# Input projections by seven block products in front, prompt heads in pairs on halves of the array, and gate and merge weights through ACT's queue

## The chip, the cores and the metric

The kernel runs on one core of a Trainium2 chip. Its time is the device time of one execution in microseconds (us). PE is the matrix engine (PEld its weight loads), DVE, ACT and POOL the vector, scalar and general engines; SP issues DMAs, and so can ACT.

## The reference, cut to what matters

One layer of a streaming encoder on 1024 prompt frames and 8 x 16 sample frames (1152 rows of 1024 features, nine row tiles of 128). Everything is fp32.

```
z = rmsnorm(x) @ w_in          # qa ka va | qb kb vb (512 columns each) | fl (8) | qm (512) | gates (3 x 1024)
qa, ka, qb, kb, qm = per-head rmsnorm of their columns; mk, mv = rmsnorm(mem) @ w_mkv
A: chunk-band attention with a learned bias, 8 heads x 64     B: causal attention with forget gates, 8 heads x 64
M: attention into 256 memory rows, 4 heads x 128              samples: the same three against 512 cached rows each
x = x + (sum over b of sigmoid(gate_b) * (o_b @ w_pb)) @ w_o
x = x + relu(rmsnorm(x) @ w_up)^2 @ w_down
```

## The kernel before, in words

Each fp32 product is made of fp32r products: an operand is split into a high part (a copy on ACT, `hilo` and `split`) and a low part (source minus high, on DVE or POOL), and hi.hi + hi.lo + lo.hi are summed in PSUM (`mm3`). The stages, in time:

- **Front.** Columns V_A, Q_A, the memory keys and values, K_A and V_B (with the eight forget columns), each as nine row tiles x 8 contraction blocks x 3 matmuls (`group`). V_B is 520 wide and goes as two banks of 260 columns, the others as one of 512. `head_norm` and `to_T` norm a tile (ACT square, DVE sum, POOL root in `rstd`, DVE scale, gain) and transpose it on PE.
- **Attention A, samples A, attention B, samples B, attention M, samples M** (`attend` with `prompt_ab`, `sample_ab`, `prompt_m`, `sample_m`). A planner (`Plan`) fixes the order here: it walks in planned time, keeps a clock for each engine from `COST`, for the DMAs in `load`, for PE in `pe.matmul`, and emits the first task whose inputs are ready; when none is, it emits one step of a **filler**. What it emits is kept in that order on every engine. The fillers are, one after another: `project` (Q_B, K_B and Q_M in halves of 256 columns, 1296 matmuls), `gates` (24 feature tiles x 72 matmuls of 384 columns), `merge` (24 x 36 of 384 columns).
- **Rest.** What is left of gates and merge, then W_o and the two feed-forward products, which the change leaves alone.

In `prompt_ab` a head is 64 wide. `prepare` loads its keys twice, one copy under the other, and its queries as 64 rows of high over 64 rows of low parts, so two 128-row matmuls give one piece of scores (`scores`: `qs` with `kh`, `qs` with `kl`). `soften` adds the bias and takes the row minimum on DVE, `exp_norm` does exp on ACT and the division; `transposes` turns the probabilities on PE and splits them (`turn`: ACT high, DVE low); `values` multiplies each 128-key block with `vs`, high and low values side by side, for the high and the low part (two matmuls of up to 256 columns), and `out` adds the two halves.

In `sample_ab`, fp32 matmuls are used as they are, on four column tiles of the array (`tile_position=(0, 32 * pr)`).

The weights of gates and merge are fetched by `staged`: one staging buffer for the gates, the DMA on SP's queue, then `split`. SP's queue carries the cached keys and values of the samples as well, in the order of the plan.

## Time and profile before

| | us |
|---|---|
| runs: median of 3 (lowest to highest) | 2049.38 (2044.78 to 2052.18) |
| profiled execution | 2052.52 |
| its span | 2050.7 |
| PE busy / weight loads busy | 1994.0 / 1817.3 |
| DVE / ACT / POOL busy | 1214.4 / 965.6 / 568.4 |

PE is busy for 97% of the span; a matmul's record lasts longer than its share of the pipeline, so the distance from one start to the next tells what one costs, and busy time only where PE stood still. The mean granted clock is 0.994 of 2.4 GHz. The chain that ended last is PE's for its last 17%, and shows nothing of the stages ahead of it.

### The profile page before, as it was taken

What the parts mean: (1) busy time and instruction counts of PE and PEld (TensorE: products, weight loads), DVE (VectorE), ACT (ScalarE), POOL (GpSimd) and SP (SyncE); (2) the same over time, 40 slices, a digit from 0 to 9 for tenths busy, and PEclk for the clock granted to TensorE, in tenths of its full rate; (3) what the DMA queues carried; (4) which work ended last, traced back from release to release, by engine and by line L of the source; (5) the groups of instructions that cost most, each with busy time, mean ns of one, the idle gap of its engine ahead of it and who ended that gap; (6) DMA issues with size and microseconds to landing.
All of it is one profiled execution on the core that took longest, in us unless ns stands there. A gap on an engine that the chain in (4) does not pass through costs nothing. (4 is left out here: it accounts for less than half of the span.)

```text
span 2050.7 us, 35667 instructions
## 1 busy us (share of the span) xinstructions
PE 1994.0 (97%) x12946; PEld 1817.3 (89%) x12946; DVE 1214.4 (59%) x2383; ACT 965.6 (47%) x1950; POOL 568.4 (28%) x650
## 2 busy tenths in 40 slices
PE   9999999999899998899999999989999999999999
PEld 7778999999599997698989997889999998888887
DVE  3444178886269882254254662696555655785775
ACT  6443268886357772254242122564444454453332
POOL 2435066664134551110021010235344431000000
PEclk9999999999999999999999999999999999999999
DMA  8453155554964437745375443225343449663463
GB/s 287 137 176 122 62 136 135 148 131 125 296 179 125 123 92 238 246 131 199 132 246 179 130 144 118 67 92 178 131 144 130 140 157 318 196 200 110 127 194 127
DMA packets 227374, 325.54 MB, mean 159 GB/s; under 512 B 48101, under 2 KB 120950, under 8 KB 227198
## 3 DMA queue, kind: packets, MB, share of 16 engines
q1 hardware_dynamic: 176888, 281.85, 43.9%
q10 hardware_dynamic: 50310, 41.42, 6.5%
q8 instruction: 102, 1.67, 0.4%
q14 instruction: 74, 0.61, 0.1%
HBM read 238.00 MB, written 85.18 MB: 158 GB/s over the span
## 5 line engine op out<-in xcount | busy, mean ns | idle before, releaser
L1625 PE MATMUL b<-r 128*128 128x512 f32 (+2 forms) x2200 | 457.5, 357 | 5.3 <-ACT r L199 3.0
L1625 PEld LDWEIGHTS b<-r 128*128 128x128 f32 x2200 | 379.7, 190 | 63.5 <-ACT r L199 3.9
L199 ACT ACTIVATE r<-fa 128x512 fp32r<-128x512 f32 (+4 forms) x264 | 212.1, 813 | 330.4 <-PE b L1625 281.2
L199 DVE TENSOR_TENSOR r<-fa,r 128x512 fp32r<-128x512 f32 (+4 forms) x264 | 271.5, 1039 | 138.9 <-ACT r L199 133.9
L210 PE MATMUL z<-hi,whi 128*128 128x384 f32 x960 | 300.4, 345 | 10.9 <-ACT whi L199 9.5
L1625 PE MATMUL b<-r,r 128*128 128x320 f32 (+1 forms) x1928 | 288.3, 299 | 4.8 <-DVE r L199 4.7
L1625 PEld LDWEIGHTS b<-r,r 128*128 128x128 f32 x1928 | 271.2, 190 | 6.6 <-DVE r L199 6.6
L210 PE MATMUL z<-hi,wlo 128*128 128x384 f32 x768 | 259.5, 338 | 0.5
L210 PE MATMUL z<-whi,hi 128*128 128x256 f32 (+2 forms) x792 | 255.7, 324 | 1.8 <-DVE lf L199 0.8
L210 PE MATMUL z<-wlo,hi 128*128 128x256 f32 (+2 forms) x792 | 248.6, 314 | 1.9 <-DVE wlo L199 0.9
L210 PE MATMUL z<-whi,lo 128*128 128x256 f32 (+2 forms) x792 | 247.4, 313 | 0.0
L199 POOL TENSOR_TENSOR fa<-fa 128x512 f32<-128x512 f32 x114 | 167.7, 1478 | 246.6 <-ACT fa L199 126.3
L210 PEld LDWEIGHTS z<-hi,whi 128*128 128x128 f32 x960 | 178.5, 189 | 20.7 <-ACT whi L199 12.1
L210 PE MATMUL z<-lo,whi 128*128 128x384 f32 x576 | 194.0, 337 | 0.0
L199 ACT ACTIVATE whi<-wst 128x512 fp32r<-128x512 f32 (+1 forms) x160 | 99.5, 629 | 195.3 <-DMA wst<-in_w_g 72.4
L210 PEld LDWEIGHTS z<-wlo,hi 128*128 128x128 f32 x792 | 150.2, 190 | 14.1 <-DVE wlo L199 3.2
L210 PEld LDWEIGHTS z<-whi,hi 128*128 128x128 f32 x792 | 149.8, 189 | 12.9 <-ACT whi L199 2.5
L210 PEld LDWEIGHTS z<-whi,lo 128*128 128x128 f32 x792 | 149.8, 189 | 9.4 <-DVE lo L199 0.4
L199 DVE TENSOR_TENSOR wlo<-wst,whi 128x512 fp32r<-128x512 f32 (+1 forms) x127 | 96.4, 771 | 102.8 <-ACT whi L199 102.1
L210 PEld LDWEIGHTS z<-hi,wlo 128*128 128x128 f32 x768 | 144.9, 189 | 2.6 <-DVE wlo L199 2.6
L199 ACT ACTIVATE s<-s,nm 128x256 f32<-128x256 f32 (+8 forms) x180 | 122.3, 681 | 41.3 <-DVE nm L199 38.3
L199 POOL TENSOR_SCALAR s<-s,ri 128x640 f32<-128x640 f32 (+8 forms) x100 | 78.1, 783 | 183.9 <-DVE ri L199 148.3
(190 smaller groups left out, 3401.8 us busy)
## 6 DMA issues: line engine op xcount, KB each, us to landing
td<-fa SPq DMA_DIRECT2D x112, 256.0 KB
fa<-td SPq DMA_DIRECT2D x80, 256.0 KB
fa<-in_w_down SPq DMA_DIRECT2D x76, 256.0 KB
fa<-in_w_up SPq DMA_DIRECT2D x32, 512.0 KB
tg<-tg ACTq DMA_DIRECT2D x72, 192.0 KB
th<-tg SPq DMA_DIRECT2D x72, 192.0 KB
wst<-in_w_in SPq DMA_DIRECT2D x48, 256.0 KB
wst<-in_w_g SPq DMA_DIRECT2D x48, 256.0 KB
```

Source lines behind the costliest of these rows:

```text
L199: ins = f(*a, **k)
L210: ins = nc.tensor.matmul(out, lhsT, rhs, **k)
L1625: pin(nc.tensor.matmul(ps, lh, rh, **k))
```

## The change

**Projections.** `project`, `group` and the fillers made of them go. V_A with the forget columns (520 wide) comes first as before V_B did. The other six column groups go in three pairs (Q_A, K_A), (V_B, Q_B), (K_B, Q_M). For a pair, an even and an odd row tile and the two halves of the contraction are a 2 x 2 block product, which `products` makes of seven block products (S1 to S4 are sums of blocks of x from `sums`, T the sums of weight blocks from the sources in `makers_of`); the ninth row tile is made straight. Weights stand in seven slots, each filled again by `release`; `in_order` keeps PE and DVE in the order written. `norm` runs in steps, each some row tiles behind (`in_`). Memory keys and values follow. All this stands ahead of attention A, and the fillers are gates and merge alone.

**Prompt heads in pairs.** In `prompt_ab` two heads lie in the two halves of the 128 rows. A piece of scores is three matmuls for each head (hi.hi, hi.lo, lo.hi) on 64 rows of the array, head by head in turn, into two banks. The values are one fp32 matmul for each head and key block, on 64 columns of the array. The transposed probabilities are one fp32 copy, on ACT or DVE.

**Queue.** `staged` issues its DMA on ACT's queue, which the planner counts apart (`dma2`). The planner also counts a matmul on a part of the array with that part's share.

```diff
-            plan.now += n * ((2 if "tile_position" in k else 4) if rhs.dtype == F32 else 2 if n < 256 else 1) / 2400 + 0.003
+            side = 128 * 128 // (lhsT.shape[0] * out.shape[0]) if "tile_position" in k else 1
+            plan.now += n * (4 if rhs.dtype == F32 else 2 if n < 256 else 1) / side / 2400 + 0.003
...
+    UW, NR, NW = HB + 8, 10, 7
+    RW, WA, SA = arena(prj, "rw", NR * UW), arena(prj, "wa", 2 * NW * UW, F32R), arena(prj, "sa", 4096, F32R)
...
+    def sums(t):
+
+        x = x_place(t)
+        e0, e1, o0, o1 = x[:, 0:4, 0:P], x[:, 4:8, 0:P], x[:, 0:4, P:], x[:, 4:8, P:]
+
+        def scale(kh):
+            y = x[:, 4 * kh:4 * kh + 4, :]
+            return lambda: vec.tensor_tensor(y, y, gcol[:, 0, 4 * kh:4 * kh + 4, None].to_broadcast((P, 4, 256)), ALU.mult)
+
+        def s1():
+            vec.tensor_tensor(o1, o0, o1, ALU.add)
+            hilo(o1, S1[:, t, 0], S1[:, t, 1])
+
+        def s2():
+            vec.tensor_tensor(o1, o1, e0, ALU.subtract)
+            hilo(o1, S2[:, t, 0], S2[:, t, 1])
+
+        def s3():
+            vec.tensor_tensor(o0, e0, o0, ALU.subtract)
+            into_odd(t, o0)
+
+        def s4():
...
+    def makers_of(pair, after):
...
+        def m2(k):
+            def source():
+                b, back = take()
+                vec.tensor_tensor(kept[k], b, kept[k], ALU.subtract)
+                back()
+                return take()
+            return source
+
...
+        queue.extend([x for k in ks for x in (R(k), L(4 + k))] + [R(4 + k) for k in ks] + [L(k) for k in ks]
+                     + [R(4 + k) for k in ks] + [R(k) for k in ks] + [L(4 + k) for k in ks])
+        makers.extend([m(k) for m in (m1, m2, m6, m7, m5) for k in ks] + [take] * 8 + [m4(k) for k in ks])
...
+    def run(u0, tiles, ks=range(4), free=True):
+
+        for x, (lhs, key, first, last, then) in enumerate(tiles):
+            put_lo()
+            if first:
+                zs[key] = zbank()
+            ps = zs[key]
+            for k in ks:
+                (h, l), (wh, wl) = lhs(k), (w[:, :HB] for w in wt[u0 + k])
+                pe.matmul(ps, h, wh, start=first and k == ks[0], stop=False, skip_group_check=True)
+                pe.matmul(ps, h, wl, start=False, stop=False, skip_group_check=True)
+                pe.matmul(ps, l, wh, start=False, stop=last and k == ks[-1], skip_group_check=True)
+                if free and x == len(tiles) - 1:
+                    release(u0 + k)
+            if then:
+                then(ps)
+            if len(ks) > 1:
+                flush()
+
...
+        r = tl(pj, (P, 8), tag="hr", bufs=4)
+
+        def sums():
+            q = tl(pj, (P, 8), tag="hss", bufs=4)
+            vec.tensor_reduce(q[:, :nh], v3(sq), AX.X, ALU.add)
+            rstd(q[:, :nh], r[:, :nh], dh)
+            gps.tensor_scalar(r[:, :nh], r[:, :nh], sc, 1.0, ALU.mult, ALU.mult)
+            in_(2, scale)
+
+        def scale():
+            zn = tl(pj, (P, HB), tag="zn") if fresh else z
+            vec.tensor_tensor(v3(zn), v3(z), r[:, :nh, None].to_broadcast((P, nh, dh)), ALU.mult)
+            if gain is not None:
+                vec.tensor_tensor(v3(zn), v3(zn), gain[:, None, :].to_broadcast((P, nh, dh)), ALU.mult)
...
+        run(u0, [(even(t), t, True, True, copy(u3[t])) for t in ts] + [(last, "s", True, False, None)])
+        run(u0 + 4, [(upper(last), "s", False, True, beside(left))]
+            + [(upper(even(t)), "y", True, True, m2(t)) for t in ts])
+        run(u0 + 8, [(of(S2, t), t, False, True, copy(u2[t])) for t in ts])
+        run(u0 + 12, [(odd_(t), t, False, True, copy(u3[t])) for t in ts])
+        run(u0 + 16, [(of(S1, t), "y", True, True, both(t)) for t in ts])
+        for t in ts:
+            if hook:
+                hook(t)
+            run(u0 + 20, [(of(S4, t), "y", True, True, plus(u2[t], lambda: right(2 * t, u2[t])))], free=False)
+            run(u0 + 24, [(last, "s", t == 0, False, None)], (t,))
+        run(u0 + 20, [(upper(last), "s", False, True, beside(right))])
+        if hook:
+            for t in ts:
+                hook(4 + t)
+        run(u0 + 28, [(upper(odd_(t)), t, False, True, copy(u2[t], lambda t=t: left(2 * t + 1, u2[t]))) for t in ts])
...
+    in_order.extend((pe, vec))
+    in_(8, rs_T)
+    for n, step in enumerate(sums(3)):
+        in_(n + 1, step)
+    products(8, q_out("a", 64), k_out("a"))
+    products(40, v_out(o["vb"], rs), q_out("b", 64))
+    products(72, k_out("b"), q_out("m", 128), at_last)
...
-        sp.dma_start(st, src)
-        t = plan.load(256)
+        act.dma_start(st, src)
+        t = plan.load(256, "dma2")
...
-        UK, NL, NS = (3, 1, 3) if b == "a" else (4, 2, 4)
+        UK, NS, NU, NB = (3, 6, 8, 3) if b == "a" else (4, 5, 7, 3)
...
+                    qh, ql, kh, kl = heads[p][:4]
+                    ks, qc, ps = slice(k0 * P + x, k0 * P + x + m), slice(blk * P, (blk + 1) * P), []
+                    for e in range(2):
+                        if x == 0:
+                            ss_[n, e] = tl(pool, (P, WK), tag="s", bufs=NS)
+                        ps.append((plan.take("s"), tl(psum["s"], (P, 512), tag="s")))
+                    for j, (q, k) in enumerate(((qh, kh), (qh, kl), (ql, kh))):
+                        for e in range(2):
+                            r = slice(64 * e, 64 * e + 64)
+                            pe.matmul(ps[e][1][:, :m], q[r, qc], k[r, ks], start=j == 0, stop=j == 2, tile_position=(64 * e, 0))
+                    for e in range(2):
+                        plan.spawn(soften(e, ps[e][1], ps[e][0], x, m, x + m == nkey))
...
+                k = plan.first(m * P, ("act", 0), ("vec", 0.2))
+                if k == "act":
+                    act.activation(dst, t[:, 0:m, :], AF.Copy)
+                else:
+                    vec.tensor_copy(dst, t[:, 0:m, :])
+                t_ = plan.op(k, m * P)
...
+                pv, vd = tl(psum["pv"], (P, 512), tag="pv")[:, 0:256], heads[p][4]
+                for m, (kb, a, z) in enumerate(plan_):
+                    for e in range(2):
+                        pe.matmul(pv[64 * e:64 * e + 64, a * P:z * P], vd[:, kb, 64 * e:64 * e + 64],
+                                  units[p, g][e][u][:, r, a * P:z * P], start=m == 0, stop=m == len(plan_) - 1, tile_position=(0, 64 * e))
...
-    plan.bufs = dict(z=2, tp=3, s=2, pv=1)
+    plan.bufs = dict(z=2, tp=2, s=3, pv=1)
```

On PE, in the projections. Before, among the fillers, one row tile of Q_B (`z`; `whi`, `wlo` are weight parts, `hi`, `lo` parts of x):

```order
L210 MATMUL z_2616<-wlo_1969,hi_145_213 128x256
L210 MATMUL z_2616<-whi_1968,lo_150_218 128x256
L217 MATMUL tp_2639<-ident_203,lf_210 72x128
L210 MATMUL z_2616<-whi_1968,hi_145_213 128x256
L210 MATMUL z_2616<-wlo_1969,hi_145_213 128x256
L210 MATMUL z_2616<-whi_1968,lo_151_219 128x256
```

Now, in the front, the product with S4 (in `sb`) of the first pair, the weights in `wa`; `fe` holds normed results on their way to a transposition:

```order
L215 MATMUL z_1629<-wa_256,sb_264 128x512 x12
L222 MATMUL tp_1646<-ident_203,fe_268 128x128 x4
L215 MATMUL z_1621<-wa_256,hi_163_231 128x512 x2
L215 MATMUL z_1621<-wa_256,lo_166_234 128x512
L215 MATMUL z_1669<-wa_256,sb_264 128x512 x12
```

1296 matmuls of 256 columns are gone from the fillers, and those of 512 columns in the front are 1248 where they were 744.

On PE, in attention A, a score piece of 512 columns. Before:

```order
L210 MATMUL s_3310<-kh_2928,qs_2930 128x512
L210 MATMUL s_3310<-kl_2929,qs_2930 128x512
```

Now:

```order
L215 MATMUL s_4185<-kh_3835,qh_3837 128x512
L215 MATMUL s_4187<-kh_3835,qh_3837 128x512
L215 MATMUL s_4185<-kl_3836,qh_3837 128x512
L215 MATMUL s_4187<-kl_3836,qh_3837 128x512
L215 MATMUL s_4185<-kh_3835,ql_3838 128x512
L215 MATMUL s_4187<-kh_3835,ql_3838 128x512
```

Two heads took four matmuls of a piece, and take six, in three rounds. In A and B together there are 96 such pieces of two heads, and PE passes 247 times between the whole array and a part of it.

On the queues, in samples A (`kd`, `vd`, `v` are cached keys and values, `wst` the gates' staging buffer). SP before:

```order
L199 DMA kd_7191<-in_cak 128x512 x4
L199 DMA kd_7271<-in_cak 128x512 x4
L199 DMA wst_7325<-in_w_g 128x512
L199 DMA kd_7364<-in_cak 128x512 x4
L199 DMA v_1780_7091<-out_va 16x512
L199 DMA vd_7392<-in_cav 128x512 x4
```

SP now, and behind it ACT a little later, in attention B:

```order
L203 DMA kd_6694<-in_cak 128x512 x4
L203 DMA kd_6747<-in_cak 128x512 x4
L203 DMA v_1240_6344<-out_va 16x512
L203 DMA vd_6813<-in_cav 128x512 x4
L203 DMA kd_6833<-in_cak 128x512 x4
```

```order
L203 ACTIVATE s_7512,sm_7597<-s_7512,nm_7567 128x896
L203 ACTIVATE s_7514,sm_7611<-s_7514,nm_7570 128x896
L203 DMA wst_7633<-in_w_g 128x512
L203 ACTIVATE pt_7584<-tp_7628 128x4x128
L203 ACTIVATE pt_7585<-tp_7643 128x4x128
```

The weights left SP's queue, and stand on ACT between the exp of the scores and the copies of the transposed probabilities. On PE, 210 matmuls of fillers stood between the first score of samples A and the first of attention B, and 318 do now; between samples B and attention M 255, and now 372.

## Rows read from the trace of the kernel before

**Rows 1.** Busy time by stage: front, A, samples A, B, samples B, the rest.

```profile
core 0: us, PE busy (x) PEld busy (x) DVE busy (x) ACT busy (x) POOL busy (x), PEclk, DMA share, GB/s
0.00:293.40 293.40, 288.15 (x1659) 248.93 (x1660) 114.91 (x198) 131.73 (x248) 105.44 (x125) 1.00 0.49 153
293.40:507.70 214.30, 212.79 (x1768) 210.63 (x1770) 177.56 (x549) 167.20 (x441) 129.74 (x186) 1.00 0.50 133
507.70:588.00 80.30, 69.71 (x712) 54.27 (x711) 23.82 (x77) 23.95 (x60) 9.21 (x18) 0.98 0.81 255
588.00:791.30 203.30, 203.11 (x1376) 197.86 (x1376) 165.74 (x462) 143.90 (x333) 95.85 (x132) 1.00 0.46 129
791.30:889.80 98.50, 83.15 (x752) 65.82 (x752) 26.22 (x79) 26.36 (x63) 8.42 (x22) 0.95 0.77 243
...
960.90:1213.10 252.20, 243.95 (x1517) 233.68 (x1517) 128.47 (x232) 70.39 (x138) 29.62 (x27) 0.99 0.55 175
```

**Rows 2.** Timeline of PE in the front: start us, duration us, instruction.

```profile
22.03 0.39 PE L210 MATMUL z<-wlo,hi 128*128 128x512 f32 x1
22.26 0.40 PE L210 MATMUL z<-whi,lo 128*128 128x512 f32 x1
```

**Rows 3.** Timeline of PE in attention A: values, then scores.

```profile
352.88 0.28 PE L210 MATMUL pv<-ptl,vs 128*128 128x256 f32 x1
353.00 0.22 PE L210 MATMUL pv<-pth,vs 128*128 128x128 f32 x1
353.05 0.28 PE L210 MATMUL pv<-ptl,vs 128*128 128x128 f32 x1
353.17 0.33 PE L210 MATMUL s<-kh,qs 128*128 128x256 f32 x1
```

**Rows 4.** Timeline of the weight loads (PEld) there.

```profile
353.00 0.19 PEld L210 LDWEIGHTS pv<-ptl,vs 128*128 128x128 f32 x1
353.11 0.19 PEld L210 LDWEIGHTS s<-kh,qs 128*128 128x128 f32 x1
```

**Rows 5.** Timeline of PE in samples A: scores, fillers, values, transpositions.

```profile
556.62 1.10 PE L210 MATMUL s<-kd,qb 128*32 128x264 f32 x16
557.65 0.44 PE L210 MATMUL z<-hi,whi 128*128 128x384 f32 x1
557.93 0.34 PE L210 MATMUL z<-lo,whi 128*128 128x384 f32 x1
558.10 0.34 PE L210 MATMUL z<-hi,wlo 128*128 128x384 f32 x1
...
558.62 0.34 PE L210 MATMUL z<-hi,wlo 128*128 128x384 f32 x1
558.89 1.08 PE L210 MATMUL pv<-vd,spt 128*32 128x128 f32 x32
559.79 0.40 PE L210 MATMUL pv<-v,t 128*32 128x128 f32 x8
560.12 0.77 PE L217 MATMUL tp<-ident,s 128*128 128x128 f32 x5
560.64 0.42 PE L210 MATMUL z<-hi,whi 128*128 128x384 f32 x1
```

**Rows 6.** What PE waited for: first line samples A, the others samples B.

```profile
PE s L210 <- DMA kd<-in_cak: 5.4, 6, 1.5
...
PE s L210 <- DMA kd<-in_cbk: 5.0, 6, 1.9
PE z L210 <- ACT whi L199: 4.4, 1, 4.4
```

**Rows 7.** Groups of DVE and POOL: busy us, mean ns, idle before and releaser.

```profile
L199 DVE TENSOR_TENSOR wlo<-wst,whi 128x512 fp32r<-128x512 f32 x119 | 88.1, 748 | 100.9 <-ACT whi L199 100.1 <-issue 0.2
...
L199 POOL TENSOR_TENSOR hr<-hr,mhalf 128x8 f32<-128x8 f32 x18 | 29.5, 1639 | 1.5
```

**Rows 8.** The gates' stores on ACT's queue: issue ns (min/median/max), first and last us.

```profile
L199 ACTq DMA_DIRECT2D tg<-tg x72: 320/326/1142, 514.6 to 1061.8; - x72
```

More of the change, by code (lines that the diff above doesn't have):

```diff
@@ L188, in tile_encoder @@
     plan = Plan()
+    in_order = []
     class Engine:
@@ new lines, in tile_encoder, with prepare, put_lo, produce @@
+    wt, makers = [], []
+    sources, los = [], []
+    def prepare(u):
+        if len(sources) <= u < len(makers):
+            sources.append(makers[u]())
+    def put_lo():
+        while los:
+            los.pop(0)()
+    def produce(place, lo_now=None):
+        u = len(wt)
+        prepare(u)
+        put_lo()
+        if u == len(makers):
+            return
+        src, then = sources[u]
+        h, l = (x[:, :src.shape[1]] for x in place)
+        act.activation(h, src, AF.Copy)
+        wt.append(place)
+        def lo():
+            (lo_now or vec).tensor_tensor(l, src, f32(h), ALU.subtract)
+            if then:
+                then()
+        los.append(lo)
+        if lo_now:
+            put_lo()
+        else:
+            prepare(u + 1)
@@ new lines, in release, with ask, take, back @@
+    def release(u):
+        if u != NW:
+            produce(wt[u])
+    queue, asked, taken, used = [], [0], [0], set()
+    def ask():
+        while asked[0] < len(queue) and (asked[0] < NR - 4 or asked[0] - (NR - 4) in used):
+            sp.dma_start(raw[4 + asked[0] % (NR - 4)][:, :HB], queue[asked[0]])
+            asked[0] += 1
+    def take():
+        n = taken[0]
+        taken[0] += 1
+        assert n < asked[0]
+        def back():
+            used.add(n)
+            ask()
+        return raw[4 + n % (NR - 4)][:, :HB], back
@@ new lines, in k_out, with then, v_out, handle @@
+    def k_out(b):
+        def then(t, zn):
+            sp.dma_start(o["k" + b][t * P:(t + 1) * P, :], zn)
+            in_(2, lambda: to_T(zn, kT[b], t))
+        return lambda t, z: norm(z, rs[:, t:t + 1], 64, lambda zn: then(t, zn), g_of["k" + b])
+    def v_out(dst, scale, fresh=False):
+        def handle(t, *of):
+            zn = of[0] if of[0].shape[1] == HB and not fresh else tl(pj, (P, HB), tag="zn")
+            x = 0
+            for z in of:
+                act.activation(zn[:, x:x + z.shape[1]], z, AF.Copy, scale=scale[:, t:t + 1])
+                x += z.shape[1]
+            act.dma_start(dst[t * P:(t + 1) * P, :], zn)
+        return handle
@@ new lines, in tile_encoder @@
+    sp.dma_start(bf, i["b_f"].to_broadcast((P, 8)))
+    x_load(4)
+    x_split(4)
+    x_load(1, slice(0, 4))
+    x_load(1, slice(4, 8))
+    x_rows(1)
+    x_split(1)
+    x_rows(TT - 1)
+    PAIRS = ((Q_A, K_A), (V_B, Q_B), (K_B, Q_M))
+    for n, pair in enumerate(PAIRS):
+        makers_of(pair, PAIRS[n + 1] if n < 2 else None)
+    queue.extend(i["w_mkv"][k * P:(k + 1) * P, x:x + HB] for x in (0, HB) for k in range(KD))
+    makers.extend([take] * 16)
+    for k in range(4):
+        sp.dma_start(kept[k], rows_(Q_A)(k))
@@ L438, in forget_gates @@
+    mem_products(104, mem_k)
+    fes.close()
+    sbs.close()
+    pgs = ExitStack()
+    pg = pgs.enter_context(tc.tile_pool(reuse_waits="tile", name="pg", bufs=2, side="right"))
+    rb = tl(pg, (P, NT), tag="rb", bufs=1)
+    sp.dma_start(rb, rsd.to_broadcast((P, NT)))
     def forget_gates(pool):
@@ new lines, in prompt_ab, with prepare, load @@
+        kq, vb, done, bias_at = Times(), Times(), Times(), Times()
+        turned, summed = defaultdict(int), defaultdict(dict)
+        live, softs = [0], [0]
+        pvs = set()
+        def prepare(p):
+            r = slice(p * P, (p + 1) * P)
+            def load(src):
+                w = yield from plan.ring(("ld", b), 1)
+                t = tl(pool, (P, NP), tag="ld", bufs=1)
+                sp.dma_start(t, src[r, 0:NP])
+                return t, plan.load(512), w
+            kd, t, w = yield from load(kT[b])
+            kh, kl, qh, ql = (tl(pool, (P, NP), F32R, tag=x) for x in ("kh", "kl", "qh", "ql"))
+            vd = tl(pool, (P, 8, P), tag="vd")
+            heads[p] = qh, ql, kh, kl, vd, {}
+            for part in range(2):
+                yield t
+                for x, n in halves(NP):
+                    c = slice(x, x + n)
+                    yield from plan.idle("act")
+                    yield from split(kd[:, c], (kh, qh)[part][:, c], (kl, ql)[part][:, c], n)
+                plan.give(w)
+                if part == 0:
+                    kd, t, w = yield from load(qT[b])
+            kq[p] = plan.t
+            sp.dma_start(vd, o["v" + b].rearrange("(k p) c -> p k c", p=P)[:, 0:8, r])
+            vb[p] = plan.load(512)
+            if p == 0:
+                plan.spawn(prepare(1))
@@ L1555, in tile_encoder @@
     plan.filler = next(f), f
-    with tc.tile_pool(reuse_waits="tile", name="fg", bufs=1) as pool:
-        plan.spawn(forget_gates(pool))
-        plan.run([])
     def attend(name, part):
```

696 lines of the change are left out of this document (320 added, 376 removed).

## The prediction

> **What bounds the kernel now.** I read busy time by stage first. PE is the bound in nearly every stage [rows 1]: in attention A it stands idle 214.30 - 212.79 = 1.5 us, in attention B 0.2 us, with DVE, the next, at 178 and 166 us. So what the change is worth is read from PE's work, matmul by matmul. The exceptions are the two sample stages [rows 1]: PE idles 80.30 - 69.71 = 10.6 us in samples A and 98.50 - 83.15 = 15.4 us in samples B, while the DMAs carry 255 and 243 GB/s. W_o and the feed-forward part follow from 1213.1 us on, and nothing changes there.
>
> Second, what a matmul costs: the distance of starts in the timeline. In the front a 512-column matmul takes 0.23 us [rows 2]. A 256-column one takes 0.12, a 128-column one 0.05 and then 0.12, 0.085 on average [rows 3]; 384 columns take 0.17 (557.93 to 558.10) [rows 5]. So a 512-column matmul costs 0.23 where two of 256 cost 0.24.
>
> Third, parts of the array. The samples' scores are eight fp32 matmuls, 16 records, on four column tiles of 32, and take 557.65 - 556.62 = 1.03 us; the values are 20 fp32 matmuls of 128 columns, 40 records, in 560.12 - 558.89 = 1.23 us [rows 5]. The tiles run side by side: a round of four values takes about 0.226 us if 0.1 goes to the passage. That passage shows too: the first filler behind the scores is followed after 0.28 us where its fellow takes 0.17, and the last filler ahead of the values after 0.27 [rows 5]. I take 0.1 us for each passage between the whole array and a part.
>
> **The change part by part.** The profiled execution took 2052.5 us, 3.1 above the median of the runs; the sum goes against it.
>
> *Projections.* Before: 744 matmuls of 512 columns, 432 of 260 and 1296 of 256. Now 1248 of 512 (96 of them the memory's, as before), and the same 432 of 260. That is 504 x 0.23 = 115.9 us more and 1296 x 0.12 = 155.5 us less: **-39.6 us**. Seven block products for eight are 30 us of it, whole banks for half ones the rest. The transpositions stay as many.
>
> *Scores.* Before: 80, 160, 112 and 32 matmuls of 512, 384, 256 and 128 columns: 80 x 0.23 + 160 x 0.17 + 112 x 0.12 + 32 x 0.085 = 61.7 us. Now 96 pieces in three rounds of two halves: 60, 120, 84 and 24 rounds. No row shows two row halves at work. Lower end: a round costs one matmul, 47.2 us (128 columns at 0.12). Upper end: the halves follow each other, 576 matmuls, 92.7 us. I take the lower end, since the four column tiles are the nearest rows: **-14.5 us**, with -14.5 and +31.0 kept.
>
> The rule that speaks against it: the Trainium skill (TensorE: Matmul & The Clock Gate, section LDWEIGHTS) gives a weight load a time of columns / 1.2 GHz, however few rows it has, so each half's load of 128 columns would be 107 ns; by that, if the loads follow each other, a round is at least 0.213 us and the scores come to 62.4 us, which is no gain. The trace agrees for the whole array, where such loads start 0.11 us apart [rows 4]; no run here shows two loads to different rows.
>
> *Values.* Before 448 matmuls of 256 columns at 0.12 and 160 of 128 at 0.085: 67.4 us [rows 3]. Now 304 fp32 matmuls in 152 rounds of two; by the samples' round 0.45 us for 256 columns and 0.226 for 128: 112 x 0.45 + 40 x 0.226 = 59.4 us, **-8.0 us**. If two tiles of 64 did not overlap it would be +51.4; four of 32 do [rows 5].
>
> *Passages.* Score pieces and value groups now stand between matmuls of the whole array: 247 passages x 0.1 = **+24.7 us**, where attention A and B had none. Ends: 0, if row halves pass freely, and 0.2 each.
>
> *DVE and ACT in A and B.* The low parts of the transposed probabilities, the joining of the two halves of the values and the second copy of the keys go. PE is the bound there, so this is worth 0; it is cover for the queue's cost below.
>
> *Fillers moved into the sample stages.* 108 more matmuls in samples A and 117 more in samples B, 225 x 0.17 = 38.3 us of work, taken from stages where PE had no idle time. Own work of a sample is 1.03 + 1.23 us and five transpositions in 0.52 [rows 5]: 2.8 us, so 22.4 us a stage, and with 210 and 255 fillers (35.7 and 43.4 us) PE had 58.1 of 80.3 and 65.8 of 98.5 us to do. 55 us are free for 38.3. What eats into it are bytes: 225 matmuls are three feature tiles with 0.5 MB of weights and 0.6 MB of results each, 3.4 MB or 13 us at 255 GB/s. Ends 0 and -38.3; I take **-30 us**.
>
> *Queue.* With the weights on ACT's queue, SP's holds only cached keys and values there; waits for the first kd of a sample (5.4 and 5.0 us) and the 4.4 us for `whi` are the most that this can free [rows 6], and they are within the 55 us above. On ACT 72 issues of some 0.33 us [rows 8], 24 us over 700, and each waits for the one staging buffer, read last by DVE or POOL (0.75 us on DVE [rows 7]). Behind it stand the exps and the copies of attention. ACT is busy 167 of 214 and 144 of 203 us [rows 1], and loses more than that with the split probabilities; PE has fillers meanwhile. Ends 0 and 15; I take **+3 us**.
>
> *The front.* DVE now makes weight sums, low parts, evictions and norms: 314 operations and 47 sums of 512 columns ahead of the first score. At 0.75 us [rows 7] these are 271 us, some 310 with the smaller ones, under PE's 377 (1248 x 0.23, 432 x 0.12, 190 transpositions at 0.11 and 102 fillers that stand ahead of the first score). PE covers it. What it costs where the cover fails is a wait for a low part or a normed tile: **+5 us**, ends 0 and 30.
>
> Sum: -39.6 - 14.5 - 8.0 + 24.7 - 30 + 3 + 5 = -59.4, so 2052.5 - 59.4 = 1993.1 for a profiled execution, and 3.1 less, **1990 us**, for the median.
>
> **The rivals.**
> - *The loads of two halves follow each other.* A round is then two loads of 0.11, 0.22 us [rows 4], for all but 512 columns: 60 x 0.23 + 228 x 0.22 = 64.0 us, +16.8, 2007 us. For it: loads of 128 columns start 0.11 us apart on the whole array [rows 4], and two matmuls of 128 columns can be 0.12 us apart [rows 3]. Against: four tiles' matmuls begin as one [rows 5].
> - *Row halves don't overlap at all*, the change not doing what it says: +45.5, 2036 us. Against: rows 5, for columns.
> - *The sample stages are DMA's.* If each byte counts, what is moved there takes its full time: +30, 2020 us. For it: 255 and 243 GB/s [rows 1], and fillers gone to where the caches are fetched. The Trainium skill (Trainium Kernel Development and Optimization, section Key Constraints) says so of the queue: all queues run on the same 16 engines, and a second one saves issue time only. No run here shows it yet. Against: PE waited 5 us a stage for kd, not 20 [rows 6].
> - *Slower: the front's fixed order.* DVE stands in written order, and a norm's scale waits there for POOL's root, 1.64 us [rows 7]. If the two row tiles between sum and scale give no cover, 47 norms cost 47 x 1.64 = 77 us, with PE waiting at the transposition, in place of the 5 us above: 2062 us. It decides from (2056 - 1985) / 47 = 1.5 us a norm on. Against: two row tiles are 24 matmuls, over 5 us.
> - *Better:* passages free and all the moved fillers covered: 1990 - 24.7 - 8.3 = 1957 us.
>
> **How the numbers follow.** Forecast 0.56, loads in turn 0.14, no overlap 0.07, DMA's 0.12, the fixed order 0.07, better 0.04. The forecast's own range is 1968 to 2012. Left out of 1955 to 2034 are the fixed order, the no-overlap case and a little below: under 0.2. A change of 0.3%, 6 us, is about what a measurement of this kernel can tell. Faster holds for all but the fixed order and half of the no-overlap case: 0.87; same 0.05; slower 0.08.
>
> **What would show it.** In the changed profile: the first score near 390 us, where PE has 377 us of work, with few waits for DVE; two score matmuls starting within some ns, rounds of 0.23 us for 512 columns (0.21 for 256 if loads take turns); attention A near 170 us, B near 205, with PE never idle; samples A near 84 and B near 100 us with idle PE of a few us; 67 us of merge (395 matmuls) behind samples M. It is wrong if samples B grows by 20 us or more, if PE waits in the front for `hr`, or if score pairs stand a full matmul apart.

## The result, and the profile after

The changed kernel takes 2027.45 us (median of 4 runs, 2023.93 to 2028.52), against 2050.55 for the kernel before on the same chip: a ratio of 0.9876, 95% interval 0.9854 to 0.9898. It is faster, by 23 us by the medians (25 by the ratio) and not by the 60 that were forecast. The profiled execution took 2028.52 us, where the sum of the steps gave 1993.1.

The busy time by stage of the changed kernel, from the same view and with the same columns as [rows 1]. The stages are the front, attention A, samples A, attention B, samples B, attention M, samples M, what is left of the merge, and W_o with the feed-forward part:

```profile
core 0: us, PE busy (x) PEld busy (x) DVE busy (x) ACT busy (x) POOL busy (x), PEclk, DMA share, GB/s
0.00:410.50 410.50, 394.72 (x2002) 331.94 (x2002) 281.43 (x500) 226.07 (x412) 149.69 (x180) 0.99 0.58 176
410.50:583.20 172.70, 172.70 (x1255) 140.01 (x1254) 98.50 (x340) 101.88 (x264) 52.76 (x73) 1.00 0.35 108
583.20:672.10 88.90, 84.78 (x817) 72.41 (x816) 27.14 (x81) 28.30 (x66) 9.74 (x19) 0.98 0.83 269
672.10:884.00 211.90, 211.90 (x1477) 172.30 (x1480) 116.71 (x351) 113.98 (x264) 75.62 (x121) 1.00 0.31 98
884.00:991.50 107.50, 98.18 (x869) 85.19 (x869) 36.35 (x99) 35.00 (x80) 11.81 (x25) 0.95 0.83 265
991.50:1063.20 71.70, 71.28 (x443) 67.61 (x442) 49.22 (x93) 39.51 (x111) 15.34 (x12) 1.00 0.57 180
1063.20:1133.80 70.60, 62.40 (x473) 54.90 (x474) 41.56 (x77) 19.00 (x43) 15.91 (x14) 0.93 0.71 241
1133.80:1190.30 56.50, 51.78 (x289) 49.60 (x288) 42.92 (x73) 18.28 (x34) 15.67 (x12) 1.00 0.50 151
1190.30:2026.70 836.40, 820.24 (x4730) 736.55 (x4728) 539.81 (x708) 360.54 (x556) 178.23 (x132) 1.00 0.47 153
```

W_o begins at 1190.3 instead of 1213.1 us and takes 836.4 instead of 837.6. So the gain lies ahead of W_o, and there in PE's busy time, 1147.7 us instead of 1172.0. PE's idle time, the first column less the second, is 42.6 us where it was 41.1. The forecast had taken 22 us off it. The samples gave some idle time back (samples A 10.6 to 4.1 us, samples B 15.4 to 9.3), but the front took 10.5 us more (5.3 to 15.8) and the end, samples M and merge, 4.7 more (8.25 to 12.9).

Busy time is not work alone. PE's clock stands at one of two levels, 2.4 or 1.2 GHz, and a matmul at the lower level is busy for longer. In samples B of the changed kernel (the granted clock is 0.50 from 941.7 us on) the first fillers behind a wait, whose starts are otherwise 0.17 us apart, stand 0.32 us apart:

```profile
940.84 1.18 PE L215 MATMUL pv<-vd,spt 128*32 128x128 f32 x32 [2.19 <-ACT spt L203]
...
942.85 0.52 PE L215 MATMUL z<-lo,whi 128*128 128x384 f32 x1
943.17 0.52 PE L215 MATMUL z<-hi,wlo 128*128 128x384 f32 x1
```

Ahead of W_o the clock was at the lower level for 17.1 us of the profiled execution before and for 34.1 us of the one now, and PE was busy for 15.7 and 31.5 us of these; so at the full clock its busy time fell by 32 us and not by 24. In both executions each fall of the clock came behind waits of PE, so a wait can cost more than its length. Executions of one kernel differ in this: the mean clock of the changed kernel's four runs is 0.990 to 0.996.

The second thing to see is in the timeline of PE in attention A, a piece of scores of 384 columns between two stretches of whole-array work, and the weight loads that belong to it (start, us, engine, line, operation, shape, count):

```profile
454.03 0.33 PE L215 MATMUL z<-lo,whi 128*128 128x384 f32 x1
454.20 0.34 PE L215 MATMUL z<-hi,wlo 128*128 128x384 f32 x1
454.47 0.45 PE L215 MATMUL s<-kh,qh 64*128 64x384 f32 x2
454.75 0.34 PE L215 MATMUL s<-kl,qh 64*128 64x384 f32 x2
454.93 0.33 PE L215 MATMUL s<-kh,ql 64*128 64x384 f32 x2
455.19 0.33 PE L222 MATMUL tp<-ident,s 128*128 128x128 f32 x1
455.45 1.30 PE L215 MATMUL pv<-pt,vd 128*64 128x256 f32 x10
...
454.03 0.19 PEld L215 LDWEIGHTS z<-hi,wlo 128*128 128x128 f32 x1
454.46 0.19 PEld L215 LDWEIGHTS s<-kh,qh 64*128 64x128 f32 x2 [0.25 <-issue]
454.57 0.19 PEld L215 LDWEIGHTS s<-kl,qh 64*128 64x128 f32 x2
```

The two halves run side by side (x2 stands on one row), and a round costs what one matmul does: 454.75 to 454.93, 0.17 us for 384 columns. But at the passage there are two delays, not one. The last filler is followed after 0.27 us where 0.17 is its share, and the first round after 0.28 where 0.17 is its share; going out, it is 0.26 for 0.17. The loads say why. Inside one shape a load starts with the matmul before it (454.03 for the matmul of 454.20). At the passage the load of the new shape starts only at 454.46, after the last filler has run its 0.17 us and 0.09 more, and the next load follows that one, so that the second round too is late by the 0.10 us of a load that nothing hides. That makes 0.2 us a passage. The Trainium skill (TensorEngine Tiling (Array Packing), section Key Properties) states that a change of the tiling mode drains the engine; the trace agrees, since the new shape's load waits until the last matmul of the old one has run.

### The profile page after: what moved, and what is told of

It is laid out like the page before. It is cut to its first block, busy times and chain, and to the rows that moved or that the text cites. A ratio compares the mean times of both kernels' runs of the same rounds, so it can differ in the third digit from the quotient of the medians.

```text
span 2026.7 us, 33952 instructions
## 1 busy us (share of the span) xinstructions
PE 1968.0 (97%) x12338; PEld 1710.5 (84%) x12338; DVE 1233.7 (61%) x2320; ACT 942.6 (47%) x1827; POOL 524.8 (26%) x587
## 5 line engine op out<-in xcount | busy, mean ns | idle before, releaser
L215 PE MATMUL z<-hi,whi 128*128 128x384 f32 x960 | 321.2, 366 | 9.4 <-ACT hi L203 4.0
L215 PE MATMUL z<-wa,hi 128*128 128x512 f32 (+1 forms) x732 | 203.7, 365 | 6.7 <-ACT hi L203 5.0
L215 PEld LDWEIGHTS z<-wa,hi 128*128 128x128 f32 x732 | 128.8, 192 | 27.6 <-ACT hi L203 5.4
L203 POOL TENSOR_SCALAR s<-s,ri 128x256 f32<-128x256 f32 (+8 forms) x105 | 77.0, 738 | 265.8 <-DVE ri L203 219.0
L203 DVE CUSTOM_DVE_ANT_0 s<-s,bias 128x384 f32<-128x384 f32 (+4 forms) x144 | 71.0, 526 | 100.5 <-PE s L215 100.0
L215 PE MATMUL z<-wa,lo 128*128 128x512 f32 (+1 forms) x366 | 130.2, 359 | 0.0
L215 PEld LDWEIGHTS z<-lo,whi 128*128 128x128 f32 x576 | 109.9, 191 | 0.0
L222 PE MATMUL tp<-ident,s 128*128 128x128 f32 (+1 forms) x680 | 102.2, 276 | 1.2 <-POOL s L203 1.2
L203 DVE TENSOR_TENSOR fa<-b,fa 128x256 f32<-128x256 f32 (+1 forms) x160 | 70.8, 450 | 52.4 <-PE b L1849 38.1
L203 DVE TENSOR_TENSOR wa<-rw,wa 128x512 fp32r<-128x512 f32 (+1 forms) x102 | 67.8, 687 | 56.3 <-ACT wa L203 56.3
```

The costliest lines, as they stand in the source:

```text
L203: ins = f(*a, **k)
L215: ins = nc.tensor.matmul(out, lhsT, rhs, **k)
L222: ins = nc.tensor.transpose(*a)
```

## The experiments

All kernels start from the changed one unless said otherwise. The table has the median, the ratio to the kernel before on the same chip with its interval, and from the view of busy time by stage, up to the start of W_o, PE's busy and idle time. These last three are of the profiled execution, which can lie off the median: 2034.6 us for e12, 2044.2 for e3, 2067.6 for e4.

| | us | ratio | W_o starts at | PE busy | PE idle |
|---|---|---|---|---|---|
| before | 2050.6 | 1 | 1213.1 | 1172.0 | 41.1 |
| changed | 2027.5 | 0.9876 (0.9854-0.9898) | 1190.3 | 1147.7 | 42.6 |
| e1 attention as before | 2025.4 | 0.9883 (0.9854-0.9911) | 1188.0 | 1131.1 | 56.9 |
| e2 queue as before | 2035.0 | 0.9927 (0.9901-0.9954) | 1195.2 | 1153.9 | 41.3 |
| e3 projections alone | 2040.1 | 0.9953 (0.9936-0.9970) | 1205.3 | 1145.2 | 60.1 |
| e4 two excursions a piece | 2063.7 | 1.0065 (1.0042-1.0088) | 1230.0 | 1190.3 | 39.7 |
| e10 one excursion, same matmuls | 2030.5 | 0.9903 (0.9889-0.9918) | 1196.0 | 1156.1 | 39.9 |
| e5 fewer passages | 2010.3 | 0.9805 (0.9786-0.9824) | 1172.2 | 1129.2 | 43.0 |
| e6 front's tail | 2030.4 | 0.9907 (0.9891-0.9923) | 1191.0 | 1148.6 | 42.4 |
| e7 e1 with six buffers | 2026.7 | 0.9885 (0.9870-0.9900) | 1187.2 | 1132.1 | 55.1 |
| e8 e5 and e6 | 2012.7 | 0.9820 (0.9799-0.9840) | 1173.9 | 1133.0 | 40.9 |
| e9 e5, more fillers in samples A | 2011.3 | 0.9805 (0.9788-0.9821) | 1173.6 | 1128.2 | 45.4 |
| e12 e7, merge's loads on POOL's queue | 2041.7 | 0.9941 (0.9922-0.9960) | 1196.9 | 1143.6 | 53.3 |
| e13 e5, merge's loads on POOL's queue | 2015.4 | 0.9818 (0.9790-0.9846) | 1175.2 | 1131.8 | 43.4 |

### The price of a passage: e4, e10, e11, e5

e4 puts one whole-array matmul of zeros into each piece of scores:

```diff
                     for j, (q, k) in enumerate(((qh, kh), (qh, kl), (ql, kh))):
+                        if j == 1:
+                            pe.matmul(ps[0][1][:, :P], zr, zr, start=False, stop=False, skip_group_check=True)
```

> The changed kernel with one whole-array matmul of 128 columns, zeros times zeros and so without effect on the sum, between the first and the second round of each score piece: 96 pieces are left and entered once more, 192 more passages. Theory P: 96 x (0.11 + 2 x 0.2) = 49 us, 2076 us. Rival: what looks like a passage is a fixed price of a group of row halves (its banks, its waits), paid once a piece: 96 x 0.11 = 11 us, 2038 us.

e10 has the same matmul at `j == 0`, with `start=True, stop=True`, so ahead of the first round. The planner puts every filler in the same place in both kernels.

> The kernel e4 with the added matmul of 128 columns ahead of the first round of a score piece instead of between the first and the second: the same matmuls and the same place of every filler, but 242 passages in attention A and B in place of 418. It prices the 176 passages alone. In the profile of e4 an added passage cost 0.15 us: 26 us less than e4's 2063.7, about 2037 us. By 0.2 us a passage it would be 35 less, 2029 us; by 0.1 us 18 less, 2046 us. If e4's loss was the added matmuls themselves: no difference, 2064 us.

Measured: 2063.7 against 2030.5 us. In the order of the instructions e4 has 433 changes of shape in attention A and B and e10 249, counting also those between halves of rows and halves of columns, which the expectations leave out. So 184 passages cost 33 us (28 to 39 by the two intervals), 0.18 us each, in kernels whose matmuls are the same. In attention A and B alone, with equal fillers, PE never idle and the clock at 1.00 in both, the two stages take 421.3 and 385.4 us, 0.195 us a passage. The 96 matmuls themselves cost 3 us by the medians and 6 by the ratios (0 to 11). The fixed price of a group falls, and so does the 0.1 us of the forecast. The two kernels in the timeline of PE, e10 first:

```profile
454.17 0.34 PE L215 MATMUL z<-hi,wlo 128*128 128x384 f32 x1
454.35 0.22 PE L215 MATMUL s<-zr 128*128 128x128 f32 x1
454.50 0.39 PE L215 MATMUL s<-kh,qh 64*128 64x256 f32 x2
454.72 0.28 PE L215 MATMUL s<-kl,qh 64*128 64x256 f32 x2
454.84 0.28 PE L215 MATMUL s<-kh,ql 64*128 64x256 f32 x2
```

```profile
452.87 0.34 PE L215 MATMUL z<-hi,wlo 128*128 128x384 f32 x1
453.14 0.33 PE L215 MATMUL s<-kh,qh 64*128 64x128 f32 x2
453.40 0.33 PE L215 MATMUL s<-zr 128*128 128x128 f32 x1
453.66 0.33 PE L215 MATMUL s<-kl,qh 64*128 64x128 f32 x2
453.82 0.27 PE L215 MATMUL s<-kh,ql 64*128 64x128 f32 x2
```

In e4 the rounds of 128 columns, whose share is 0.11 us, stand 0.26 us from the matmul between them, on either side. e10 shows in passing what a round of 256 columns costs once the shape is set: 454.72 to 454.84, 0.12 us.

e11, three such matmuls in place of one, was run once:

> The kernel e4 with three added matmuls in place of one between the first and the second round. In e4 the lone matmul between two passages took 0.15 us a passage, where passages that whole-array work follows take 0.2 (0.1 in front of the first instruction behind it and 0.1 in front of the second). If the second 0.1 belongs to the passage, it shows again here, at the step from the first to the second added matmul; the time is then e4's plus 96 x (2 x 0.11 + 2 x 0.05) = 31 us, 2095 us. Rival: a passage costs 0.15 whatever follows; then 21 us, 2085 us.

It took 2080.9 us, 17 more than e4, below both figures, and PE's idle time shrank beside it (39.7 to 34.5 us), so the time decides nothing. Its starts show the second delay (0.16 us from the first added matmul to the second, 0.11 from there to the third); for 128 columns it is 0.05 and not 0.10.

e5 keeps the matmuls and changes their order. All pieces of a block are emitted together, with four score banks; values share the transposed tiles' two banks; and the planner prefers a ready task of the shape that PE is in:

```diff
-    plan.bufs = dict(z=2, tp=2, s=3, pv=1)
+    plan.bufs = dict(z=2, tp=2, s=4)
...
-            return [(*piece(x, m), ("s", n)) for x, m in pieces]
+            return [(ready, emit, ("s", n))]
...
+                    part = self.pairs and chain[0] in "sv"
+                    cost = 0 if part == self.part else 1
```

> The changed kernel with the same matmuls in another order: both pieces of a block of scores directly behind each other (four banks for scores, the values share the two banks of transposed tiles), and a group of values behind scores where both are ready. In the order of the instructions the passages between whole array and halves go from 238 to 126. Theory P (0.2 us a passage, PE full in attention A and B): 112 x 0.2 = 22 us less, 2005 us. By the forecast's 0.1 us: 11 us less, 2016 us. Rival: the passages stand where PE would otherwise wait for a bank or a softmax, and with the coarser order it waits there instead: 2020 to 2030 us with idle PE in A and B.

Measured: 2010.3 us, 17 less than the changed kernel by the medians, 15 by the ratios. Counted with the changes between the two kinds of halves, 247 passages became 159, so 88 and not 112 went: 0.17 to 0.19 us each, the price of e4 and e10 again. In attention A and B alone, again at a clock of 1.00, PE is busy for 15 us less once e5's 66 fewer fillers there are counted, 0.17 us a passage. PE waited little for the coarser order:

```profile
411.40:578.70 167.30, 166.85 (x1270) 143.69 (x1269) 99.73 (x340) 101.91 (x260) 56.40 (x79) 1.00 0.36 112
663.30:856.50 193.20, 191.05 (x1392) 160.26 (x1391) 111.22 (x349) 110.99 (x258) 74.54 (x119) 1.00 0.32 102
```

PE is idle 0.5 us in attention A and 2.2 in B. This version is faster than both kernels.

### The parts alone: e1, e2, e3

e1 puts back the earlier `prompt_ab` and its banks (`dict(z=2, tp=3, s=2, pv=1)`), e2 the earlier queue, e3 both:

```diff
-        act.dma_start(st, src)
-        t = plan.load(256, "dma2")
+        sp.dma_start(st, src)
+        t = plan.load(256)
```

> The changed kernel with the earlier prompt attention of heads A and B (one head at a time, scores and values as matmuls of the whole array, banks 3 for transposed tiles and 2 for scores); projections and queue stay changed. Theory P, passages: in attention A and B of the changed profile the rounds themselves are cheap (scores 46.6 us, values 55.0 us) but each passage between whole array and part costs 0.2 us and not 0.1, 46 us in both stages. Taking all this back costs 61.7 - 46.6 + 67.4 - 55.0 = 27.5 us of matmuls and saves 46: 18.5 us less, about 2009 us. Rival Q, the passages are hidden or go elsewhere and the paired rounds are a gain: 2027.5 + 27.5 = 2055 us. Rival R, ACT and DVE, which get the splits of the probabilities back, become the bound in A and B: no gain, 2020 to 2035 us with PE idle there.

> The changed kernel with the weights of gates and merge loaded through SP's queue again. By the forecast's term the ACT queue costs 3 us, so 2024 us. Rival: the ACT queue is what lets the sample stages take more fillers than before; without it SP's waits for cached keys and for weights (10.4 and 4.4 us before) come back and more with the 225 added matmuls: 2035 to 2042 us, seen in samples A and B. Third: it makes no difference, 2027 us, and what the sample stages don't absorb is set by something else.

> Attention and queue as before, only the projections (and with them the place of the fillers) changed. If the two parts add up: 2009 us by theory P plus or minus what the queue alone does. If the earlier attention, which issues more DMAs on SP (two loads a tensor and head), needs the queue to be free, this is slower than the sum of the two by 5 us or more.

The projections alone gain 10 us by the ratio (2040.1) and not 40. PE's busy time falls by 27 us in the profiled execution; it was at the lower clock for 47.8 us there, 40.7 of them busy, and at the full clock the fall is 39 us, the forecast's term. 19 us come back as idle time: 12.4 in the front, 6.6 in samples B and next to nothing in samples A. e3 is slower than e1 and e2 add up to by 7 us by the medians and 4 by the ratios, which doesn't settle whether the earlier attention needs SP's queue free.

e1's time, 2025.4, lies in the range of rival R, but not for its reason, and theory P's 2009 was missed. PE's busy time falls by 16.6 us against the changed kernel, near what theory P has (18.5), but the idle time grows by 14.3, and not in A and B, where rival R had it (1.2 and 1.3 us), but in samples B:

```profile
906.60:1015.20 108.60, 80.93 (x750) 65.17 (x750) 35.98 (x97) 29.18 (x68) 11.00 (x24) 0.86 0.81 255
```

27.7 us idle there, against 9.3, and the clock is at 0.86. So the pairing costs PE 14 us in attention A and B (busy time there, less that of the different fillers, at a clock of 1.00 in both) and gives about as much back by leaving more gates for the samples (1014 fillers in A and B, where e1 uses 1260).

The queue is a gain, not a cost: without it 7.5 us are lost beside the paired attention (e2; 10 by the ratios), and 15 beside the earlier one (e3 against e1). That is the lower edge of what e2's rival had, and the samples do wait more, but not as it had it: PE waits 3.1 us for cached keys there (5.2 in the changed kernel) and 5.6 for the weights (`whi`). e2's samples:

```profile
583.40:661.10 77.70, 67.92 (x682) 52.74 (x681) 22.54 (x73) 24.33 (x58) 10.00 (x19) 0.91 0.86 285
873.00:969.20 96.20, 82.85 (x767) 67.83 (x767) 25.34 (x78) 27.46 (x64) 9.78 (x24) 0.93 0.77 245
```

They hold 453 fillers in place of 690 and are 22.5 us shorter for it; but 237 fillers are 41 us of PE elsewhere. 11 of the 19 us between come back in samples M and the merge (127.1 us for 552 fillers in the changed kernel, 154.4 for 774 here). In e2's profiled execution the idle time up to W_o is no longer than in the changed kernel, and of its 6 us more of busy time some 4 are the lower clock (0.91 and 0.93 in the rows above). Which change of the order costs this was not tried.

### Where a gain goes: e7, e9, e12, e13

In e1 the gates run out at 924 us, in the middle of samples B, and the merge's first operands (`oTa`) stand on SP's queue among the caches:

```profile
919.57 1.32 SPq L203 DMA_DIRECT2D wst<-oTa  x3
...
921.64 4.86 SPq L203 DMA_DIRECT2D kd<-in_cbk  x4
...
931.96 0.33 SPq L203 DMA_DIRECT2D wst<-oTa  x1
...
925.68 0.58 ACT L203 ACTIVATE spt<-tp 128x512 f32<-128x512 f32 x1
933.36 0.34 ACTq L203 DMA_DIRECT2D wst<-in_w_pa  x1
933.80 0.27 ACT L203 ACTIVATE t<-tp 16x128 f32<-16x128 f32 x1 [7.54 <-DMA vd<-in_cbv]
```

The first three operands are issued at 919.6, the fourth 12 us later. And ACT does nothing from 926.3 to 933.4: the issue of a merge weight stands in its order there, ahead of the copy `t`. By the trace's semaphores the issue waits for a counter that DMAs of several queues use in turn. The last DMA ahead of it on this counter is a load of cached values (`vd`), issued on SP's queue at 927.95 and counted to its end at 933.28. So the issue waits for that load, as the row names it. This is a wait on ACT like the one that the forecast's queue term feared, 7 us long, though for another reason, and I took it first for one on the three staging buffers. e7 gives e1 six of them (`("st", 6)` for `("st", 3)`):

> The kernel e1 (attention as before) with six staging buffers in place of three for the merge's operands and weights. In e1 attention A and B lost their passages, 42 us, for 27 us of added matmuls, but PE waited 35 us in samples B against 16: the gates ran out at 924 us, and the merge's operands came through three buffers behind the caches on SP's queue, ACT's queue waiting for the same buffers. If the buffers are the cause, the 19 us come back: about 2008 us. Rival: SP's queue, in order behind the loads of the caches, or the transfers are the cause and not the buffers: 2020 to 2026 us.

2026.7 us, no gain: the buffers are not the cause (samples B idle 24.1 us; the expectation's 35 and 16 us are PE's waits added up in another way, and the rows have 27.7 and 9.3, the same 18 to 19 apart). e12 takes e7 and loads the merge's operands and gate values through POOL's queue (`gps.dma_start` for `sp.dma_start`, planned as a queue of its own); e13 does the same to e5, with the six buffers.

> The kernel e7 (attention as before, six staging buffers) with the merge's operands and gate values loaded through POOL's queue instead of SP's. In e1 and e7 the gates run out early in samples B, and PE then waits for the merge's first operands, 30 to 35 us in all, with 10 merge matmuls a us missing between 925 and 970 us. If these loads are late because they stand behind the cached keys and values in SP's queue, they come early now and most of the 15 to 19 us above the changed kernel's wait comes back: 2008 to 2012 us. If the transfers themselves (250 to 280 GB/s there), or the splits on ACT and DVE, set it: 2022 to 2028 us. Against it: POOL waits for staging buffers in its own order now, and its scaling of the softmax behind that: up to 2035 us.

> The kernel e5 with the same loads through POOL's queue and six staging buffers. PE waited 16.7 us in samples M and 3.4 us in the merge behind it, and 5.5 us in samples B. If SP's order is the cause, half of these 26 us come back: 1997 us. If not: 2010 us; if POOL is held up by its queue: 2015 us and more.

e12 is slower, 2041.7 us (the profiled execution took 2034.6), slower than all that its expectation names, and still answers the question. Its samples B, samples M and merge:

```profile
910.60:1024.90 114.30, 103.46 (x882) 87.82 (x882) 43.70 (x112) 33.29 (x77) 40.06 (x75) 0.99 0.88 290
1103.60:1132.20 28.60, 15.90 (x209) 8.91 (x208) 5.36 (x19) 5.90 (x18) 7.25 (x13) 0.74 0.75 272
1132.20:1196.90 64.70, 59.25 (x289) 56.63 (x290) 48.14 (x80) 22.42 (x44) 26.82 (x37) 0.88 0.47 139
```

Samples B idle 10.8 us where e1 had 27.7 and e7 24.1, so SP's order was the cause of more than half of the wait there, and the transfers were not: more is moved, at 290 GB/s, in about the same time. But the fillers that samples B took are missing in samples M, which has none left and idles 12.7 of its 28.6 us, and the merge behind it waits and runs at a granted clock of 0.88. e13 has little to gain in samples B, where e5 idles 3.4 us; samples M idles 9.7 us where e5 has 12.7, and the time is no better (2015.4, its interval overlaps that of e5). Its expectation gives such a time to POOL being held up, which was not looked into.

e9 moves fillers into samples A by planning with slower queues:

```diff
-        self.busy[queue] = max(self.busy[queue], self.t) + max(0.45, kb / (350 if queue == "dma" else 350))
+        self.busy[queue] = max(self.busy[queue], self.t) + max(0.45, kb / 280)
```

> The kernel e5 planned with 280 in place of 350 KB a us for each queue, which changes nothing but the order: 393 fillers in samples A and 381 in samples B in place of 312 and 393, taken from the end. If the sample stages had time to spare, 81 more fillers there are free: 81 x 0.174 = 14 us less than e5's 2010.3, 1996 us. If their transfers set the pace (every kernel so far moves 250 to 285 GB/s there, and samples A grew by 0.06 to 0.08 us for each added filler), it is 81 x 0.1 = 8 us, 2002 us, or nothing where PE waits for the caches: 2010 us.

2011.3 us, nothing. Samples A and B of e9, and samples A of e5 last:

```profile
580.70:678.30 97.60, 95.17 (x892) 84.36 (x891) 30.07 (x85) 32.04 (x73) 11.48 (x21) 1.00 0.77 256
873.00:993.90 120.90, 102.17 (x878) 87.60 (x878) 38.81 (x102) 35.31 (x79) 12.11 (x25) 0.93 0.77 240
```

```profile
578.70:663.30 84.60, 81.45 (x811) 70.19 (x810) 26.62 (x81) 28.11 (x65) 9.76 (x19) 1.00 0.87 282
```

81 more fillers made samples A 13.0 us longer, 0.16 us each, nearly the 0.174 that one costs, at a lower rate of transfer (256 for 282 GB/s). So PE is as good as full there from some 300 fillers on, and the DMAs are not. Samples B then ran out of gates as in e1, and idled 18.7 us.

### The front's tail: e6, e8

At the end of the changed kernel's front PE waits for the normed keys of the memory. e6 paces these norms by single steps of k (`if k % 2 or u0 == 112:` for `if k % 2:`), e8 does it to e5.

> The changed kernel with the norms of the memory's keys paced by one step of k instead of two in the last product, so that their transpositions stand before its last 12 matmuls and not behind them. If the waits at the end of the front (1.4, 2.1 and 1.4 us at 379 to 386 us of the changed profile and the slower matmuls behind them) come from this order, the first score is 5 us earlier and the time 2022 us. Rival: the gate weights, which are loaded and split there, or the root on POOL are late anyway and the wait only moves: 2027 us, 0 to 2 us.

> e5 and e6 together. If the two add up: 22 + 5 = 27 us less than the changed kernel, 2000 us; without the tail's part 2005 us.

No gain: 2030.4 and 2012.7 us, 3 and 2 us more than without it. The first score comes at 412.7 us instead of 410.5. PE's longest wait in the front from 370 us on, in e6:

```profile
PE tp L222 <- DVE zn L203: 6.6, 1, 6.6
```

The transpositions stand earlier in PE's order, but the norm is no earlier, so three waits at transpositions (4.7 us in all) became one of 6.6 us. In the changed kernel ACT waits 3.64 us there for the first gate weights (`whi<-wst`) and copies `hi<-rw` only behind that; the low parts on DVE wait for `hi`, and the norm's sum stands behind them in DVE's written order. What one would gain by freeing this chain was not tried.

## Why the prediction was wrong

The direction, the chance for it and the outer range (1955 to 2034) held. The size did not: 2027 lies outside the forecast's own 1968 to 2012, and no rival explains it. The profiled execution is 35.4 us above the sum. Two terms account for more than that, and others for some of it the other way.

**The passages, mis-sized: +20 us.** The mechanism and the number (247) were right, and the upper end that was kept, 0.2 us, is near the value. 247 x 0.18 = 45 us where 24.7 stood; the delays added up over all of them, by the distances of starts in the changed trace, are 45.0 us too. The step that failed was the reading of [rows 5]: the 0.28 us behind the scores and the 0.27 ahead of the values are two delays of one kind at two different passages, and I took one of them for the whole price. A passage shows one delay ahead of its first instruction and another ahead of the second. e4, e10 and e5 put the price at 0.17 to 0.2 us in the time, not only in the trace.

**The idle time, +23.5 us.** -30 (fillers moved into the samples), +3 (queue) and +5 (front) should have given -22, and gave +1.5.
- *"55 us are free for 38.3"* was wrong from its own rows: PE was idle 10.6 + 15.4 = 26 us in the two stages [rows 1]. By the sum it was to be busy for 58.1 + 65.8 us there, and was for 69.7 + 83.2. The 2.8 us for a sample's own work was read from inside its fp32 stretches and left out their passages, which are in [rows 5]: 70 in the two stages, some 13 of these 29 us. The rest was not traced. The fillers came (108 and 117 more, as forecast) and took back 12.5 us where 30 stood: 17.5 us, the other step that failed. The samples grew by 8.6 and 9.0 us. e9 shows that samples A has next to no room for more.
- *The front* idles 10.5 us more, not 5. It is not the norms as a whole: waits for normed tiles (`zn`) are 2.8 us. The waits of the changed kernel's front, the longest four:

```profile
PE z L215 <- ACT hi L203: 5.0, 2, 2.6
PE tp L222 <- DVE zn L203: 2.8, 2, 1.7
PE z L215 <- DVE wa L203: 2.3, 3, 1.3
PE tp L222 <- DVE lf L203: 1.9, 1, 1.9
```

  `hi` are the high parts of x, at 22 and 44 us, behind ACT's other work at the start; PE's clock falls to the lower level at 23.5 and 44.0 us. No run changed this part of the front, so its cause is read from the waits alone.
- *The queue* cost nothing that shows and gained 7.5 us (e2). The term took the gain for part of the 55 us and priced ACT's issues; the samples without the second queue idle 9.7 us more (e2).
- *The end* was not in the sum at all: samples M and merge idle 4.7 us more.

**The clock, not in the sum: +8 us in the profiled execution.** PE was busy for 31.5 us at the lower level where it had been for 15.7, and half of that time is lost. As the executions differ in it, this part is partly chance.

**The other terms.** Projections: the spacings hold (0.23 and 0.12), -39.6 stands (e3 has 39 at the full clock); but what they were worth alone was 10 us (e3), because the front and samples B waited more and the clock fell with it. Scores now: the rounds came to 60 x 0.23 + 120 x 0.174 + 84 x 0.115 + 24 x 0.109 = 47.0 us, for 47.2. Scores before were put too low: by the distances of starts in the trace before they took 70 us and not 61.7, because the first matmul of a piece is often followed late. The one that starts at 353.17 [rows 3] has 256 columns and was taken at 0.12 us, and the next starts 0.17 us behind it:

```profile
353.34 0.28 PE L210 MATMUL s<-kl,qs 128*128 128x256 f32 x1
```

So scores fell by 23 us and not by 14.5. Values: a round of 256 columns is two steps of 0.216, 57.1 us in all, -10.3 for -8.0. With the passages, scores and values together are a loss of PE time: -33 + 45 = +12 us, near the 14 that e1 shows in attention A and B. The corrections are +20 (passages), +23.5 (idle), +8 (clock), -9 (scores), -2 (values) and -1 (W_o), 40 us for the 35.4; the rest was not traced.

**The rivals.** *Loads of two halves in turn* is out: the loads of a pair start together, and a round of 256 columns takes 0.12 us. The rule of the Trainium skill on loads (TensorE: Matmul & The Clock Gate, section LDWEIGHTS), applied to the two halves one after the other, gave an estimate of 0.213 us, and the trace does not bear that out. *No overlap* is out by the same rows. *The samples are DMA's* looked right by the time, 2020 us, and is wrong by the mechanism: samples A is full of PE's work (e9), and in samples B of e7 more than half of the wait was SP's order (e12). What the 9.3 us are that the changed kernel's samples B waits was not tried. *The fixed order* costs no 1.64 us a norm, as PE waits 2.8 us in all for normed tiles. *Better* is out, since passages are not free.

What was to be seen: the first score came at 410 and not near 390 us; attention A took 173 for 170, B 212 for 205, with PE never idle; samples A 89 for 84 and B 107.5 for 100; the merge behind samples M 56.5 for 67; score pairs stand side by side. None of the three signs of being wrong came: what failed were sizes and the free time, not the overlap of the halves.

## What to carry to other kernels

Count how often PE changes between whole-array and partial matmuls before packing small ones: at 0.18 us a change, here, a piece of three rounds loses more by its two passages than the pairing saves, unless pieces stand together, and putting them together gained 15 us without a matmul less. Read the free time of a stage as the idle time in its own row, not as its length less a sum of starts. And a gain in a stage whose gaps are filled from a stock of other work is paid out only if the stock lasts to the stages that wait: follow the fillers to where they run out. Where PE waits, look at its granted clock too: here it fell behind waits, and the matmuls that followed took up to twice their time.

## What the hardware did that was not expected

A passage has two delays of about 0.10 us, one in front of the first instruction of the new shape and one in front of the second (0.05 where the first has 128 columns, and between the fp32 records of the values). Straight from column halves to row halves, eight times in the changed kernel, it is the same: 0.21 us where the last record of values has 0.11 for its share, and then 0.28 for 0.17 (384 columns). Otherwise the row halves don't hold each other up: loads and matmuls of a pair start together, and a round costs one matmul down to 128 columns (0.11 us). And moving loads to another queue helped by what no longer stands in line: in e12's samples B the queues together moved 290 GB/s, where the 255 GB/s of e1 had looked like the DMAs' own limit. A DMA issue on ACT waited 7 us for a load of SP's queue that used the same counter, and held up ACT's own work (e1).
